# Unused matmuls of twelve kinds in front of every second feature-major block of a decoder trunk

## The chip, the cores and the metric

The kernel runs on one NeuronCore of a Trainium2 chip. The metric is the device time of one execution in microseconds (us); the median of three runs stands for a version.

## The reference

A trunk of two decoder layers on 256 positions of width 2048, all in float32. A layer is two residual steps:

```
proj  = rms_norm(x, norm1_w) @ w_in                 # 2048 -> 6400
mixed = [retention | dilated attention | gMLP]      # 768 + 768 + 512, each normalised
x     = x + mixed @ w_out                           # 2048 -> 2048
h     = rms_norm(x, norm2_w) @ w_up                 # 2048 -> 11264
x     = x + (silu(gate) * val) @ w_down             # conv of width 3 over h, 5632 -> 2048
```

A final RMSNorm follows the second layer. Nearly all arithmetic is in the four projections.

## The kernel before, in words

Every projection is done in three terms. An activation tile `x` is a float32r pair: `xh`, the rounded value, in columns 0 to 255, and `xl`, the remainder, in columns 256 to 511. A weight piece (128 rows x 1024 columns of float32) comes by DMA into `raw`; ScalarE writes its rounded part `hi` (L113) and VectorE the remainder `lo` (L123), both float32r. The product is hi·xh + hi·xl + lo·xh, three matmuls into one PSUM tile.

`proj_t` (L335 and after) computes feature-major blocks: one block is 128 output features by all 256 positions. For each of its 128-row slices k, `W.take` hands out the next 128 columns of `hi` and `lo`; these are the stationary operand, the 256 columns of `x` are the moving one, and L352 issues the three matmuls. So a block of w_out or w_up (16 slices) has 48 matmuls, and one of w_down has 48, 48 or 36 (three parts of 16, 16 and 12 slices). The first four blocks of a call (`lead`) are interleaved in groups of eight slices, as their inputs become ready; the others run one after the other. The accumulators are four PSUM tiles with the tag `mm`.

`proj_n` (L381 and after) does the position-major parts of w_in with the roles swapped: `x` is stationary, `hi` and `lo` are moving (L392).

All other matmuls of the kernel (attention, retention, gMLP, the sums of the norms, the transposes) write to a second set of four PSUM tiles, tag `mx`, got by `mx()`. They are slipped between two weight pieces of the main stream: at the start of each piece `W.take` calls `step`, which advances one stage of each waiting evacuation (`ev`) and of up to three background generators (`bg`), and splits the piece that will be needed three pieces later. The order on each engine is thus the order in which the Python program issues the instructions; there is no scheduler behind it. In plain float32 (not float32r) a matmul appears as two MATMUL instructions, each with its own weight load; a transpose and a float32r matmul appear as one.

The lines that the texts below name: L113 and L123 (the split of a weight piece), L352 (the feature-major stream), L392 (the position-major stream), L307 and L317 (sums and broadcast of a norm, float32, with `ones` and `diag`), L424 and L425 (attention scores, float32, 128 and 256 columns), L440 (transposes of attention), L447 to L449 (attention times values, float32, 128 columns), L410 (transposes of the mixer outputs), L479, L480 and L489 to L491 (retention). `ident` is a 128x128 identity and `ones` a 128x128 tile of ones, both float32.

Of the kernel before, what the change touches and what calls it, by code (L numbers as in the profile page):

```python
# [27 lines left out]
P = 128  # L28
D = 2048
S = 256  # L30
# [12 lines left out]
PIECE = 1024  # L43
# [27 lines left out]
class Weights:  # L71
# [48 lines left out]
    def split_lo(self, p, halves=(0, 1)):  # L120
        hi, lo, src = self.parts[p]
        for h in self._halves(p, halves):
            self.nc.vector.tensor_tensor(lo[:, h], src[:, h], hi[:, h].bitcast(F32), op=ALU.subtract)  # L123
        if p % PPC == PPC - 1 and 1 in halves:
            self.loaded.pop(p // PPC)
            if p >= 2:
                self.load(p // PPC + RAW + 1)

    def take(self, mat, l, row, col, width):
        p, off = divmod(self.pos, PIECE)  # L130
        if off == 0:
            new = list(range(self.nsplit, min(p + (self.ahead if p >= 8 else 2 if p else 1) + 1, self.npieces)))
            self.nsplit += len(new)
            if p < 8:
                for q in new:
                    self.split_hi(q)
                    self.split_lo(q)
                self.step(0)
                self.step(1)
            else:  # L140
                self.step(0)
                self.step(1)
                for q in new:
                    self.split_hi(q)
                    self.split_lo(q)
            self.parts.pop(p - 1, None)
        assert off + width <= PIECE
        self.plan.append((mat, l, row, col, width))
        self.pos += width
        hi, lo, _ = self.parts[p]  # L150
        return hi[:, off : off + width], lo[:, off : off + width]


def trunk_kernel(tc, x0, xt, stream, par, cst, wst, lnw, out):
# [3 lines left out]
    V, A, T, GP = nc.vector, nc.scalar, nc.tensor, nc.gpsimd  # L158
    ctx = ExitStack()
    with ctx:  # L160
# [38 lines left out]
        def run(g):  # L199
            ev.append(g)  # L200

        W = Weights(nc, stream, raw, hp, lp, 3, step)
        live = [0]

        def mm():
            until(lambda: live[0] < 4)
            live[0] += 1
            return ps.tile([P, 512], F32, name="mm", tag="mm")

        def mt():  # L210
            return mm()[:, 0:S]

        def mx():
            return ps.tile([P, 512], F32, name="mx", tag="mx")
# [16 lines left out]
        ident = cp.tile([P, P], F32, name="ident")  # L231
        make_identity(nc, ident)
        ones = cp.tile([P, P], F32, name="ones")
# [26 lines left out]
        def operand(j, wcol):  # L260

            w = first[:, j : j + 1] if wcol == C_N1 else prm[:, wcol + j : wcol + j + 1]
            p = pp.tile([P, 2 * S], F32R, name=f"p{j}", tag=f"p{j}")
            split_hi(p, X[j], w)
            yield
            split_lo(p, X[j], w)
            PX[j] = p
# [67 lines left out]
        def proj_t(mat, l, rows, cols, opnd, evac, lead):  # L335


            n = len(rows)
            groups = [list(range(lead))] + [[m] for m in range(lead, len(cols))]
            for g in groups:  # L340
                fast[0] = lead > 0 and W.pos > 0 and (len(g) > 1 or g[0] == len(cols) - 1)
                acc = {m: mt() for m in g}
                sz = 8 if len(g) > 1 else n
                for k0 in range(0, n, sz):
                    for m in g:
                        for k in range(k0, min(k0 + sz, n)):
                            x = opnd(k)
                            hi, lo = W.take(mat, l, rows[k], cols[m], P)
                            xh, xl = x[:, 0:S], x[:, S : 2 * S]
                            terms = ((hi, xh), (hi, xl), (lo, xh)) if l == 0 else ((hi, xh), (lo, xh), (hi, xl))  # L350
                            for i, (w, v) in enumerate(terms):
                                T.matmul(acc[m], w, v, start=k == 0 and i == 0, stop=k == n - 1 and i == 2)  # L352
                        if k == n - 1:
                            run(evac(m, acc[m]))

        def moved(acc):

            t = temp()
            A.activation(t, acc, AF.Copy)
            live[0] -= 1  # L360
            return t
# [44 lines left out]
        def mixed_block(slot, l, src, c0):  # L406

            t = mx()
            for j in range(2):
                T.transpose(t[:, j * P : (j + 1) * P], src[j][:, c0 : c0 + P], ident)  # L410
            q = qp.tile([P, 2 * S], F32R, name=f"q{slot}", tag=f"q{slot}")
            w = prm[:, C_MIX + l * NK + slot : C_MIX + l * NK + slot + 1]
            yield
            split_hi(q, t[:, 0:S], w)
            split_lo(q, t[:, 0:S], w)
            QX[slot] = q
# [189 lines left out]
        for l in range(DEPTH):  # L606
# [8 lines left out]
            def att_qk(m, acc):  # L615
# [3 lines left out]
                yield from scaled(acc, aqk[h][:, half * S : (half + 1) * S])  # L619

            proj_t("w_in", l, allrows, [c + h * P for h in range(H) for c in (AQ, AK)], p_of, att_qk, 4)
            fast[0] = False

# [18 lines left out]
            def ret_qk(m, acc):  # L642
# [12 lines left out]
                V.tensor_tensor(o, o, sw, op=ALU.add)  # L655

            proj_t("w_in", l, allrows, [c + h * P for h in range(H) for c in (RQ, RK)], p_of, ret_qk, 0)

            rv = pair("rv", 768)
# [28 lines left out]

            PX[:] = [None] * NK
            proj_t("w_out", l, MIX_ROWS, [m * P for m in range(NK)], q_of, ev_out(C_N2 + l * NK), 4)  # L690

            norm["ready"] = False
# [147 lines left out]
```

## Time and profile before

| | |
|---|---|
| median of three runs | 2307.31 us (2307.05 to 2308.6) |
| the profiled execution's own time | 2307.94 us |
| its span, first to last instruction | 2306.1 us |
| granted TensorE clock, mean | 0.998 |
| TensorE matmuls, weight loads | 19430 and 19430 |
| VectorE, ScalarE busy | 63% and 50% |

How to read it: PE is TensorE's matmul, PEld its weight load, DVE is VectorE, ACT ScalarE, POOL GpSimd, SP SyncE. Matmuls are pipelined: the time that one lasts (some 280 ns) is more than twice the time from one start to the next, so a sum of durations is no time of the stream. The chain that ended last gives, for each run of matmuls of one line, how long the stream stayed there; this time divided by the count is the step from matmul to matmul. Where the stream changes its line the boundary of two pieces of the chain can be off by a tenth of a microsecond.

### The profile page before, as it was taken

What the parts mean: (1) busy time and instruction counts of PE and PEld (TensorE: products, weight loads), DVE (VectorE), ACT (ScalarE), POOL (GpSimd) and SP (SyncE); (2) the same over time, 40 slices, a digit from 0 to 9 for tenths busy, and PEclk for the clock granted to TensorE, in tenths of its full rate; (3) what the DMA queues carried; (4) which work ended last, traced back from release to release, by engine and by line L of the source; (5) the groups of instructions that cost most, each with busy time, mean ns of one, the idle gap of its engine ahead of it and who ended that gap; (6) DMA issues with size and microseconds to landing.
All of it is one profiled execution on the core that took longest, in us unless ns stands there. A gap on an engine that the chain in (4) does not pass through costs nothing.

```text
span 2306.1 us, 45994 instructions
## 1 busy us (share of the span) xinstructions
PE 2288.8 (99%) x19430; PEld 2286.0 (99%) x19430; DVE 1444.7 (63%) x2086; ACT 1142.3 (50%) x1616; POOL 24.3 (1%) x38
## 2 busy tenths in 40 slices
PE   8999999999999999999999999999999999999998
PEld 8999999999999999999999999999999999999997
DVE  6465566677547775577655655667775577656765
ACT  6465555555435553455534645545544455434554
POOL 0000100000000000000000001000000000000000
PEclk9999999999999999999999999999999999999999
DMA  7545445555555555555555455555555555555553
GB/s 285 192 154 186 165 172 186 190 184 187 188 185 189 185 178 197 177 198 183 184 194 181 158 181 173 179 184 187 184 182 192 175 200 185 189 186 186 189 183 119
DMA packets 117135, 425.15 MB, mean 184 GB/s; under 512 B 12992, under 2 KB 12992, under 8 KB 116800
## 3 DMA queue, kind: packets, MB, share of 16 engines
q1 hardware_dynamic: 116928, 422.21, 53.5%
q8 instruction: 152, 2.49, 0.4%
q14 instruction: 55, 0.45, 0.1%
HBM read 420.06 MB, written 2.10 MB: 183 GB/s over the span
## 4 chain that ended last, share of the span: by engine, by line
PE 99%; DMA 0%; DVE 0%; SPq 0%; ACT 0%; POOLq 0%; issue 0%; DVEq 0%
PE mm L352 84%; PE mm L392 12%; PE mx L410 0%; DMA xg<-in_xt_dram 0%; PE mx L425 0%; PE mx L479 0%; DVE xg L750 0%; PE mx L307 0%; PE mx L440 0%; PE mx L544 0%; PE mx L490 0%; PE mx L449 0%; PE mx L448 0%; PE mx L491 0%; PE mx L489 0%; PE mx L480 0%
## 5 line engine op out<-in xcount | busy, mean ns | idle before, releaser
L123 DVE TENSOR_TENSOR lo<-raw,hi 128x1024 fp32r<-128x1024 f32 (+1 forms) x793 | 970.0, 1224 | 745.1 <-ACT hi L113 744.1
L113 ACT ACTIVATE hi<-raw 128x1024 fp32r<-128x1024 f32 (+1 forms) x793 | 836.7, 1057 | 920.6 <-PE mm L352 505.2
L352 PE MATMUL mm<-p,hi 128*128 128x256 f32 x7168 | 1280.4, 281 | 5.9 <-ACT hi L113 5.0
L352 PEld LDWEIGHTS mm<-p,hi 128*128 128x128 f32 x7168 | 1099.3, 188 | 7.1 <-ACT hi L113 5.0
L352 PE MATMUL mm<-p,lo 128*128 128x256 f32 x3584 | 1001.8, 280 | 0.0
L352 PE MATMUL mm<-q,hi 128*128 128x256 f32 x3840 | 679.9, 280 | 0.0
L352 PEld LDWEIGHTS mm<-p,lo 128*128 128x128 f32 x3584 | 673.6, 188 | 0.5 <-DVE lo L123 0.2
L352 PEld LDWEIGHTS mm<-q,hi 128*128 128x128 f32 x3840 | 586.4, 188 | 0.0
L352 PE MATMUL mm<-q,lo 128*128 128x256 f32 x1920 | 535.9, 279 | 0.0
L352 PEld LDWEIGHTS mm<-q,lo 128*128 128x128 f32 x1920 | 360.0, 187 | 0.0
L392 PE MATMUL mm<-hi,p 128*128 128x256 f32 x1664 | 270.3, 279 | 0.0
L392 PEld LDWEIGHTS mm<-hi,p 128*128 128x128 f32 x1664 | 230.1, 188 | 0.0
L392 PE MATMUL mm<-lo,p 128*128 128x256 f32 x832 | 178.8, 277 | 0.0
L714 ACT ACTIVATE a<-hs,prm 128x256 f32<-128x256 f32 x176 | 103.9, 590 | 64.0 <-DVE hs L366 64.0
L392 PEld LDWEIGHTS mm<-lo,p 128*128 128x128 f32 x832 | 133.2, 188 | 0.0
L717 DVE SCALAR_TENSOR_TENSOR a<-hs,prm,a 128x256 f32<-128x256 f32 x176 | 85.3, 485 | 6.3
L716 DVE SCALAR_TENSOR_TENSOR a<-hs,prm,a 128x256 f32<-128x256 f32 x176 | 84.3, 479 | 4.4 <-ACT a L714 4.4
L682 DVE TENSOR_TENSOR xg<-xg,mm 128x256 f32<-128x256 f32 x128 | 53.4, 418 | 49.0 <-PE mm L352 48.8
L366 DVE TENSOR_TENSOR hs<-mm,rbc 128x256 f32<-128x256 f32 x176 | 73.6, 418 | 3.4 <-PE mm L352 3.4
L720 ACT ACTIVATE a<-a 128x256 f32<-128x256 f32 x88 | 35.6, 404 | 30.4 <-DVE a L717 30.4
L276 ACT ACTIVATE t<-xg 128x256 f32<-128x256 f32 x75 | 30.1, 408 | 40.1 <-DVE xg L682 39.2
L726 ACT ACTIVATE q<-a 128x256 fp32r<-128x256 f32 x88 | 35.5, 403 | 3.5 <-DVE a L723 3.5
(119 smaller groups left out, 581.0 us busy)
## 6 DMA issues: line engine op xcount, KB each, us to landing
raw<-in_stream_dram SPq DMA_DIRECT2D x791, 512.0 KB, 3.5
out_dram<-xg SPq DMA_DIRECT2D x8, 256.0 KB, 2.4
xg<-in_xt_dram SPq DMA_DIRECT2D x3, 512.0 KB, 8.9
cs<-in_cst_dram SPq DMA_DIRECT2D x1, 1216.0 KB, 8.4
raw<-in_stream_dram SPq DMA_DIRECT2D x2, 256.0 KB, 4.0
ws<-in_wst_dram SPq DMA_DIRECT2D x2, 256.0 KB, 4.7
lw<-in_lnw_dram SPq DMA_DIRECT2D x2, 256.0 KB, 4.9
prm<-in_par_dram SPq DMA_DIRECT2D x1, 412.0 KB, 5.8
```

The costliest lines, as they stand in the source:

```text
L113: self.nc.scalar.activation(hi[:, h], src[:, h], AF.Copy)
L123: self.nc.vector.tensor_tensor(lo[:, h], src[:, h], hi[:, h].bitcast(F32), op=ALU.subtract)
L276: A.activation(sq, X[j], AF.Square)
L352: T.matmul(acc[m], w, v, start=k == 0 and i == 0, stop=k == n - 1 and i == 2)
L366: V.tensor_tensor(out, acc, norm["bc"], op=ALU.mult)
L392: T.matmul(acc[j][:, c], v, w[:, c], start=k == 0 and i == 0 and c.start == 0, stop=k == NK - 1 and i == 2, skip_group_check=True)
L682: V.tensor_tensor(X[m], X[m], acc, op=ALU.add)
L714: A.activation(a, hs[:, 2 : S + 2], AF.Identity, scale=conv_col(ch, 2), bias=conv_col(ch, 3))
L716: V.scalar_tensor_tensor(a, hs[:, 1 : S + 1], conv_col(ch, 1), a, op0=ALU.mult, op1=ALU.add)
L717: V.scalar_tensor_tensor(a, hs[:, 0:S], conv_col(ch, 0), a, op0=ALU.mult, op1=ALU.add)
L720: A.activation(a, a, AF.Silu)
L726: A.activation(q[:, 0:S], a, AF.Copy)
```

## The change

In `proj_t`, every block that is not of the lead group, whose index is even, and whose matrix is not w_in, gets one more matmul in front of its first one. Its kind is the next entry of the list `EXTRA`, 48 entries long, which is gone through round and round. The target is a new `mx` tile that nobody reads.

```
+    def piece(self):
+        return self.parts[(self.pos - 1) // PIECE][0]
...
+                if len(g) == 1 and mat != "w_in" and g[0] % 2 == 0:
+                    extra = EXTRA[nextra[0] % len(EXTRA)]
+                    nextra[0] += 1
+                else:
+                    extra = None
...
                             hi, lo = W.take(mat, l, rows[k], cols[m], P)
                             xh, xl = x[:, 0:S], x[:, S : 2 * S]
+                            if extra and k == 0:
+                                spare(extra, hi, x)
...
+        EXTRA = (2, -256, 128, 512, -1, 64, 320, -128, 192, 264, 384, 0)
+        EXTRA = EXTRA + EXTRA[::-1] + EXTRA[::2] + EXTRA[1::2] + EXTRA[::3] + EXTRA[1::3] + EXTRA[2::3]
+        nextra = [0]
+
+        def spare(n, hi, x):
+            t = mx()
+            if n > 0:
+                T.matmul(t[:, 0:n], hi, x[:, 0:n], start=True, stop=True)
+            elif n == 0:
+                T.transpose(t[:, 0:P], ident, ident)
+            elif n == -256:
+                T.matmul(t[:, 0:S], x[:, 0:P], W.piece()[:, 0:S], start=True, stop=True)
+            else:
+                T.matmul(t[:, 0 : -n], ident, ones[:, 0 : -n], start=True, stop=True)
```

A positive entry n takes the stationary `hi` that the block's first matmul takes too, and the first n of the 512 columns of `x` (float32r). -256 swaps the roles as `proj_n` does: 128 columns of `x` are stationary, the first 256 of the weight piece are moving. -1 and -128 are plain float32 with `ident` and 1 or 128 columns of `ones`; 0 is a transpose of `ident`.

## Rows read from the trace of the kernel before

**Rows 1.** The page: busy time by engine, and the granted clock in 40 slices

```profile
PE 2288.8 (99%) x19430; PEld 2286.0 (99%) x19430; DVE 1444.7 (63%) x2086; ACT 1142.3 (50%) x1616; POOL 24.3 (1%) x38
PEclk9999999999999999999999999999999999999999
```

**Rows 2.** Waits of TensorE: engine, line, waited for, us in total, times, longest

```profile
PE mm L352 <- ACT hi L113: 5.0, 1, 5.0
PE mx L317 <- DVE diag L314: 1.7, 1, 1.7
PE mm L352 <- ACT p L254: 0.9, 1, 0.9
PE mx L307 <- ACT t L276: 0.8, 1, 0.8
```

**Rows 3.** The chain, long pieces of the two main streams: start, length, line, matmuls

```profile
79.87 32.65 PE mm L392 x288
...
414.12 743.41 PE mm L352 x6312
...
1555.30 737.77 PE mm L352 x6264
```

**Rows 4.** The chain from 112 to 135 us, attention beside L352

```profile
116.00 0.22 PE mx L424 x2
116.22 0.43 PE mx L425 x2
...
119.48 0.22 PE mx L424 x2
119.70 0.43 PE mx L425 x2
120.14 2.83 PE mm L352 x24
122.97 0.33 PE mx L440 x3
123.29 2.73 PE mm L352 x24
126.02 0.33 PE mx L440 x3
126.35 2.83 PE mm L352 x24
```

**Rows 5.** The chain from 300 to 330 us, transposes of the mixer outputs

```profile
313.09 0.22 PE mx L410 x2
313.31 2.73 PE mm L352 x24
316.03 0.44 PE mx L410 x4
316.47 5.66 PE mm L352 x48
```

**Rows 6.** The chain in the second layer, after L440 and after L410

```profile
1264.47 2.73 PE mm L352 x24
...
1454.48 2.73 PE mm L352 x24
```

**Rows 7.** Weight loads in order of time around L307: start, length

```profile
409.70 0.30 PEld L307 LDWEIGHTS mx<-ones,sqacc 128*128 128x128 f32 x2
409.92 0.30 PEld L307 LDWEIGHTS mx<-ones,t 128*128 128x128 f32 x2
410.14 0.30 PEld L307 LDWEIGHTS mx<-ones,sqacc 128*128 128x128 f32 x2
410.37 0.30 PEld L307 LDWEIGHTS mx<-ones,t 128*128 128x128 f32 x2
410.59 0.30 PEld L352 LDWEIGHTS mm<-p,hi 128*128 128x128 f32 x2
```

**Rows 8.** One long stretch by engine: length, busy times, granted clock, DMA

```profile
420.00:1150.00 730.00, 730.00 (x6201) 730.00 (x6200) 480.75 (x684) 353.75 (x464) 0.00 (x0) 1.00 0.55 187
```

**Rows 9.** Groups of TensorE's instructions: line, form, count, busy, mean ns of one

```profile
L352 PE MATMUL mm<-p,hi 128*128 128x256 f32 x7168 | 1280.4, 281 | 5.9 <-ACT hi L113 5.0 <-ACT p L254 0.9
...
L440 PE MATMUL mx<-ident,s 128*128 128x128 f32 x36 | 5.9, 272 | 0.0
```

## The prediction
> **What bounds the kernel now.** Read the busy times first [rows 1]: TensorE's matmuls and its weight loads are both at 99%, VectorE at 63%, ScalarE at 50%, and the clock is full in every slice. Then the waits [rows 2]: TensorE waits 8.4 us in all, 5.0 of it for the first weight piece, and nothing in between but for the norms. So the time is a count of matmuls times a step, and the view that gives the step is the chain. Its long pieces [rows 3] show two different steps for matmuls of the same size: L352 goes at 743.41 / 6312 = 117.8 ns (and at 737.77 / 6264 = 117.8 in the second layer), L392 at 32.65 / 288 = 113.4. I call these the long and the short step. The 280 ns that one lasts [rows 9] is no step.
>
> The short step is no privilege of L392. After three transposes, L352 runs 24 matmuls in 2.73 us (113.8 each); three more transposes later, the next 24 take 2.83 (117.9) [rows 4]. It happens again at 313.31 [rows 5], and both come back at the same places of the second layer [rows 6]. In the whole chain L352 is resumed 48 times behind other matmuls, and these four times are the only ones with the short step. Nothing waits in these pieces, the clock is the same, the operands are the same: the stream has two rhythms, holds the one it has until something foreign stands in it, and after that may be in the other. In the long stretch it holds the long one through 6312 matmuls. This decides what the change is worth, since the change puts 124 foreign matmuls into just that stretch.
>
> **The count.** Blocks behind the lead group with an even index: 6 of w_out, 14 + 14 + 10 of w_up, 3 x 6 of w_down, 62 a layer, 124 in all. Two rounds of 48 and 28 more entries give 11 of each of 2, 128, -1 and 320, and 10 of each other kind. Nothing is removed; no DMA, no VectorE or ScalarE work is added.
>
> **The cost of each.** TensorE has no idle time to hide them, so each costs its own step.
> - 2, 64, 128, 192, 264 (52 of them): bound by the load of 128 weight columns. The nearest row is a one-column float32 matmul: two passes in 0.22 us, so 0.11 for a load with hardly anything streaming [rows 7]; from the other side the 256 columns at 0.118 [rows 3]. As weights and position are those of L352, I take 0.118: 6.1 us. At 0.110 it would be 5.7.
> - Per column: L425's pass is 0.215 us, L424's 0.110 with half as many columns [rows 4]. A float32 pass of 128 columns takes the time of 256 single-pass ones (the same 0.11 that L392 nearly needs for 256), so the 128 more are 256 column times in 0.105 us, 0.41 ns each. 264 columns are then 0.11 and stay under the load; 320 are 0.136 (11 of them, 1.5 us), 384 are 0.163 (10, 1.6 us), 512 are 0.216 as L425's pass (10, 2.2 us).
> - -256 is one L392 matmul, between 0.113 and 0.118: 10 x 0.116 = 1.2 us.
> - -1 and -128 are two passes: 0.22 each [rows 4, 7], 21 of them, 4.6 us.
> - 0 is one transpose: 0.33 / 3 = 0.11 [rows 4], 10 of them, 1.1 us.
>
> Sum: 6.1 + 1.5 + 1.6 + 2.2 + 1.2 + 4.6 + 1.1 = 18.3 us. The lower bound (every one-pass kind but the three wide ones at 0.110) is 17.7. The upper one comes from a doubt: no row shows a float32r matmul narrower than 256 columns. Should it go at the float32 rate of four column times, as L424's two passes do for 128 columns (0.22), then 128 costs 0.22 and 192 costs 0.32, in place of 0.118: 11 x 0.10 + 10 x 0.20 = 3.1 more, 21.4 us.
>
> A rule of the Trainium skill would make the narrow ones cheaper: "TensorE: Matmul & The Clock Gate", section "Back-to-back issue gap", has some 60 cycles (25 ns) for up to 64 columns and 134 cycles (56 ns) for 128. By it 2, 64 and 128 would save 32 x some 0.08 us, 2.5 us of the sum. The page calls this the isolated gap, without the weight load; the one-column passes of this trace, each with its load, stand 0.11 us apart [rows 7], so the trace does not agree for this stream. The same page, "Part 4: PE-mode transpose", puts a 128x128 transpose at about 275 ns in a kernel; that is what one lasts here too (272 ns [rows 9]), but its step is 0.11 [rows 4]. By 275 the ten would cost 1.7 us more.
>
> **Waits and buffers.** The extra matmul stands at a block's first slice, often at a piece's first columns, and takes over the wait for `hi`; the three matmuls behind it in TensorE's queue need the same `hi`. The stream waits for no weight piece after the start [rows 2], so nothing is late. The `mx` tile is free: in these stages only the two norms of a layer use that tag. The evacuations come 0.1 to 0.2 us later for VectorE and ScalarE, which are busy 481 and 354 of 730 us there [rows 8]. If the weight split were close behind the stream, TensorE would wait; at 66% it isn't.
>
> **What the rhythm gives back.** L352 matmuls from the first extra of a layer to the layer's end: 576 of w_out, 4224 of w_up, 2112 of w_down, 6912, twice 13824. Each is 4.4 ns shorter at the short step (117.8 - 113.4): 60.8 us if all were. Each extra stands in front of about 111 of them, worth 0.49 us, against its own price of 0.15. So the change breaks even where the short step holds in 18.3 / 60.8 = 30% of the stretch. The only estimate for that share which rows give is 4 of 48 resumptions, 8%: 5.1 us. Net 18.3 - 5.1 = 13.2 us. On the profiled execution's 2307.94 that is 2321.1; the median of the runs lies 0.6 lower, so I forecast 2320.
>
> **Rivals.**
> - *The narrow or the odd ones set the short step* (the other side). The 48 resumptions are all behind float32 matmuls or transposes, after which the stream changes its mode. Nine of the twelve kinds are float32r and leave the mode alone; a matmul whose stream ends long before the next load frees the two from each other, and -256 is of the kind in which L392 keeps the short step for 288 matmuls. If five of the twelve leave the short step behind, it holds in some 42%: 18.3 - 25.5 = -7, 2300. It decides from 30% on. For it: the long L352 piece is undisturbed, so no row says what such a matmul does to it. Against it: 44 of 48. Chance 0.18 for faster than break-even by over 4.6 us (a share over 38%).
> - *A draw*: a quarter to a third of the stretch goes at the short step, 18.3 - 0.29 x 60.8 = +1, 2309. Same reasons, one or two kinds fewer. Chance 0.22.
> - *Narrow float32r runs in four column times*: 21.4 - 5.1 = +16, 2324. For it: float32 does. Against: an instruction of 256 float32r columns shows one pass. Chance 0.08.
> - *It isn't there*: the unread results could be left out in the build. Then 2307.3. The kernel's lines are issued by hand and nothing reads them away. Chance 0.02.
>
> **How the numbers follow.** My forecast, the long step in most of the stretch (a share under 23%, from +18 to over +4.6 us, 2312 to 2326), has 0.50. The range: up, no short step at all gives 2325.6 and the float32 rate on top a little more, so 2327; down, it cuts into the first rival at a share of 45%: 18.3 - 27.4 = -9, 2298. About 0.2% (4.6 us) is what a measurement of this kernel can tell from no change. Slower by more: 0.50 + 0.08 = 0.58; within: 0.22 + 0.02 = 0.24; faster: 0.18.
>
> **What would show it.** The chain between 330 and 1155 us falls into pieces at each extra. Right: nearly all L352 pieces have 117.8 ns a matmul, the extras 0.11 to 0.22 us. Wrong in the price: steps behind 128 and 192 of over 0.2 us, or starts 25 ns behind the 2-column ones. Wrong in the rhythm: pieces of 96 matmuls in 10.9 us where the long step gives 11.3; then the kind in front of them tells which matmul sets the rhythm, and whether the same kind always does. Anything waited for in the stretch would refute the part on waits.

## The result, and the profile after

The changed kernel takes 2324.04 us (median of three, 2323.81 to 2324.54) where the kernel before took 2307.31: 16.7 us more, a ratio of 1.0071 (95% interval 1.0049 to 1.0094). I had forecast 2320, slower. The direction and its cause stand, but one term was three times too large, one kind of the list is never issued, and the thing I called a rhythm turned out to be worth more than the whole change: set on purpose, it makes the kernel 54 us faster than before. All times here are of executions at a granted clock of 0.997 or 0.998; one of six of the version with fourteen extras ran at 0.85 and took 2470.45 us, and it is left out.

The line of the changed kernel that answers to [rows 1] stands here; TensorE's waits are the four of [rows 2], 7.9 us in all, none of them in the stretch where the extras stand.

```profile
PE 2305.9 (99%) x19565; PEld 2301.9 (99%) x19565; DVE 1445.1 (62%) x2086; ACT 1143.0 (49%) x1616; POOL 25.2 (1%) x38
```

19565 - 19430 = 135 more matmuls. By form they are 83 of hi with x, 10 of x with hi, 22 of `ones` with one column, 20 with 128. No transpose is among them: `if extra and k == 0` is false for the kind 0. Ten of the 124 places are empty, so the change has eleven kinds, not twelve, and 114 extras.

The chain from 325 us on (start, length, line, matmuls; L362 is the stream that was L352, L374, L378 and L380 are the extras):

```profile
336.75 0.00 PE mx L374
336.75 11.41 PE mm L362 x96
348.16 0.12 PE mx L378
348.28 11.30 PE mm L362 x96
359.59 0.06 PE mx L374
359.64 11.36 PE mm L362 x96
371.00 0.24 PE mx L374
371.24 11.31 PE mm L362 x96
382.55 0.12 PE mx L380 x2
382.66 11.42 PE mm L362 x96
394.08 0.03 PE mx L374
...
440.89 0.22 PE mx L380 x2
441.11 10.89 PE mm L362 x96
451.99 0.09 PE mx L374
452.08 11.33 PE mm L362 x96
```

Each price is read from the start of one extra to the start of the next, since the border behind an extra is off by some 0.1 us. 96 long steps are 11.31 us. The 2-column extra and its 96 take 348.16 - 336.75 = 11.41, so it costs 0.10; -256 costs 0.12, 128 columns 0.10, 512 columns 0.24, -1 costs 0.22. Means over all extras of a kind, from the starts of the single matmuls in the trace: 2, 64, 128 and 192 columns 0.110 to 0.111 us, -256 0.116, 264 0.121, 320 0.145, 384 0.175, 512 0.237, -1 and -128 0.224. Times their counts (11 or 10) this is 17.4 us.

At 440.89 stands a float32 extra of 128 columns, and the 96 matmuls behind it take 10.89 us: 113.4 ns each, the short step of [rows 3 to 6]. Then the 192-column extra at 451.99 ends it. This happens four times in 114, three times behind -1 and once behind -128, with 360 matmuls in all: 360 x 4.44 ns = 1.6 us given back. 17.4 - 1.6 = 15.8; of the other 0.9 us, 0.3 is at the start (the first norm's matmuls at 33.59 us, before at 33.32) and 0.5 in the last broadcast (1.21 us, before 0.68), neither of them next to an extra.

### The profile page after: what moved, and what is told of

It reads as the page before. It is cut to its first block, busy times and chain, and to the rows that moved or that the text cites. A ratio compares the mean times of both kernels' runs of the same rounds, so it can differ in the third digit from the quotient of the medians.

```text
span 2322.8 us, 46250 instructions
## 1 busy us (share of the span) xinstructions
PE 2305.9 (99%) x19565; PEld 2301.9 (99%) x19565; DVE 1445.1 (62%) x2086; ACT 1143.0 (49%) x1616; POOL 25.2 (1%) x38
## 4 chain that ended last, share of the span: by engine, by line
PE 99%; DMA 0%; DVE 0%; SPq 0%; ACT 0%; POOLq 0%; issue 0%; DVEq 0%
PE mm L362 84%; PE mm L418 12%; PE mx L374 0%; PE mx L436 0%; DMA xg<-in_xt_dram 0%; PE mx L451 0%; PE mx L505 0%; DVE xg L776 0%; PE mx L310 0%; PE mx L466 0%; PE mx L570 0%; PE mx L380 0%; PE mx L320 0%; PE mx L517 0%; PE mx L474 0%; PE mx L475 0%
## 5 line engine op out<-in xcount | busy, mean ns | idle before, releaser
L362 PE MATMUL mm<-p,hi 128*128 128x256 f32 x7168 | 1287.7, 281 | 5.5 <-ACT hi L113 5.1
L362 PEld LDWEIGHTS mm<-p,hi 128*128 128x128 f32 x7168 | 1102.4, 188 | 7.2 <-ACT hi L113 5.1
L362 PE MATMUL mm<-p,lo 128*128 128x256 f32 x3584 | 1002.8, 280 | 0.0
L362 PE MATMUL mm<-q,hi 128*128 128x256 f32 x3840 | 684.6, 280 | 0.0
L362 PEld LDWEIGHTS mm<-p,lo 128*128 128x128 f32 x3584 | 674.0, 188 | 0.7 <-DVE lo L123 0.2
L362 PEld LDWEIGHTS mm<-q,hi 128*128 128x128 f32 x3840 | 588.4, 188 | 0.1
L362 PE MATMUL mm<-q,lo 128*128 128x256 f32 x1920 | 536.3, 279 | 0.0
L362 PEld LDWEIGHTS mm<-q,lo 128*128 128x128 f32 x1920 | 360.3, 188 | 0.0
L392 DVE TENSOR_TENSOR hs<-mm,rbc 128x256 f32<-128x256 f32 x176 | 73.6, 418 | 3.4 <-PE mm L362 3.4
```

What stands on the lines that cost most here:

```text
L392: V.tensor_tensor(out, acc, norm["bc"], op=ALU.mult)
```

## The experiments

**Parts of the change alone.** Same places and order, only one family of kinds issued.

```
-                    extra = EXTRA[nextra[0] % len(EXTRA)]
+                    kind = EXTRA[nextra[0] % len(EXTRA)]
                     nextra[0] += 1
...
+                    extra = kind if kind not in (-1, -128, 0) else None   # f32r_only
+                    extra = kind if kind in (-1, -128) else None          # f32_only
```

(The comments name the run that has the line; in both, `None` means no extra.)

> Only the 93 float32r extras of the change, at their places; the 21 float32 ones are left out. Theory (each extra costs its own step, and only float32 ones can bring the short step): prices read from the changed kernel are 0.110 us for 2, 64, 128 and 192 columns, 0.116 for -256, 0.121 for 264, 0.145 for 320, 0.175 for 384, 0.237 for 512; sum 12.7 us over the kernel before, and no piece of the stretch at the short step. Rival (float32r extras set the short step too, and the float32 ones among them took it away again): some pieces of 96 matmuls in 10.9 us, and under 12 us more than before.

Measured: 2320.54 us against 2307.53, ratio 1.0055 (1.0041 to 1.0069), 13.0 us more; no new piece at the short step. The theory of the prices is right to 0.3 us.

> Only the 21 float32 extras (-1 and -128) of the change, at their places. Theory (the stream holds the rhythm that it has until the next foreign matmul, and a float32 one leaves the short step behind in about one case of five): 21 x 0.224 = 4.7 us of price, but now some 660 L352 matmuls follow each, so that each short piece gives 2.9 us; four of them give 11.7 back: 7 us faster than before, with one short piece more or less moving it by 3. Rival 1 (the short step in L352 dies out by itself within a hundred matmuls or so): 4 x 0.4 = 1.7 back, 3 us slower than before. Rival 2 (the short pieces of the changed kernel came from the other extras around them): none, 4.7 us slower.

Measured: 2259.71 against 2307.53, ratio 0.9793 (0.9779 to 0.9806): 47.8 us *faster*. All three expected numbers were wrong, that of the theory included. The chain of this kernel shows why (L378 are its extras):

```profile
424.94 14.72 PE mm L362 x125
439.66 0.22 PE mx L378 x2
439.88 97.93 PE mm L362 x864
537.81 0.22 PE mx L378 x2
538.03 32.65 PE mm L362 x288
570.67 0.12 PE mx L378 x2
570.79 9.29 PE mm L362 x81
```

The extra at 439.66 brings the short step: 97.93 / 864 = 113.3 ns. The next ones, at 537.81 and 570.67, do *not* end it; the longest piece is 1152 matmuls in 130.57 us. Of the 21 extras, five met the long step and three of them left the short one; sixteen met the short step and all sixteen left it as it was. Behind the extras 11808 matmuls go short: 11808 x 4.44 ns = 52.4 us, less 21 prices of 0.225 = 4.7, gives 47.7. Only the norms' groups of float32 matmuls end it, at 1132.58 and 1526.01 us. So what kept the change slow was not that float32 extras seldom bring the short step, but that a float32r extra follows each and ends it.

**Which float32 groups bring it.** Groups in front of even blocks, the 320-column float32r extra in front of odd ones, behind the lead group throughout. In the names T is a transpose and N with a number a float32 matmul of so many columns.

```
+                    extra = 320
+                    if g[0] % 2 == 0:
+                        extra = EXTRA[nextra[0] % len(EXTRA)]
...
+        EXTRA = ("T", "TT", "N1", "N128", "TTT", "N2", "N1N1", "N256", "TTTT", "N64", "TN1")
```

> In front of every even block one of eleven float32 groups (1 to 4 transposes; one or two matmuls of 1, 2, 64, 128 or 256 columns; a transpose and a matmul), in a mixed order, and in front of every odd block the 320-column float32r extra, which ended the short step each time that it met it. Theory (whether the stream comes out short depends on where in a fixed grid of time the group ends, so on its length and on where the stream stands): no kind always, some kinds in a third or more of their 11 places, others never; on the whole 15 to 30 of the 124 blocks behind a group at 113.3 ns a matmul, all 124 blocks behind a 320 at 117.8. Rival (a float32 group of any kind draws the rhythm with the same odds, one in five): all kinds between 0 and 5 of 11.

Measured: short behind 28 of 124 groups: one matmul of 1, 2 or 64 columns 6 of 11 each, of 128 columns 3 of 12, three transposes 3 of 11, two transposes and TN1 2 of 11 each; never behind one or four transposes, two one-column matmuls, or 256 columns. The kinds are not alike, as the rival had it. That their length decides is argued, not shown: one matmul of 1 column and one of 128 both take 0.22 us and brought it 6 of 11 and 3 of 12 times. The 320-column extra ended all 28.

**Which float32r widths bring it.** The same places, with a width from a list in front of even blocks and 320 columns in front of odd ones.

```
+        EXTRA = (322, 330, 326, 334, 324, 332, 328)      # survey_width
+        EXTRA = (312, 336, 344, 352, 360, 392, 296)      # survey_16
```

> In front of every even block a float32r extra of 322, 324, 326, 328, 330, 332 or 334 columns in a mixed order, in front of every odd block one of 320. 16 columns are the 6.67 ns in which the starts of the stream come round (three long steps are 353.3 ns, 53 x 6.67; one short one 113.3, 17 x 6.67). Theory (the start of the next matmul within these 6.67 ns decides): a wide extra sets that start by its columns, so one or two of the seven widths leave the short step behind nearly every time and the others never; blocks of 48 then in 5.44 us, not 5.65. Rival (only a change between float32 and float32r can bring the short step): no block at the short step, all seven widths alike but for 0.42 ns a column.

```profile
643.59 0.14 PE mx L374
643.74 5.65 PE mm L363 x48
649.39 0.15 PE mx L374
649.54 5.44 PE mm L363 x48
654.98 0.14 PE mx L374
655.12 5.65 PE mm L363 x48
```

The extra at 649.39 has 328 columns: 5.44 us for 48, the short step. 328 did so in 17 of 18 places; the miss, at 429.97 us, is the only one of them with a norm between it and the 320-column extra before it. The six other widths did so in none of 106. Two columns more or less, 0.8 ns at the 0.41 ns a column of [rows 4], decide here, and the rival (only a change of type can do it) is refuted.

> As the survey of widths, with 312, 336, 344, 352, 360, 392 and 296 columns in front of the even blocks and 320 in front of the odd ones. Theory (what counts is the columns modulo 16, as 16 columns are 6.67 ns): 312, 344, 360 and 392, which are 8 more than a multiple of 16 as 328 is, leave the short step behind in nearly all their places; 336 and 352 never do; 296 is 8 more too, but its stream of 0.123 us is hardly longer than a long step, so it may be set by the load instead and fail. Rival (328 is special by itself): none of them does.

Measured: 312 columns bring the short step in 17 of 17 places; 344, 360 and 392 never (0 of 54), nor 336, 352 and 296. So "columns modulo 16" holds for 312 and 328 and fails above them and at 296, which had been given a reason to fail. What singles these two out stays open.

**328 in front of every even block.**

```
+                extra = 328 if len(g) == 1 and mat != "w_in" and g[0] % 2 == 0 else None
```

> 328 columns in front of every even block, 124 of them, where the change has its mixed list. Theory (the start within the 6.67 ns decides; 328 columns carry the start of the long step onto that of the short one, and so must carry the short one's off it): the pieces between extras alternate, one at 113.3, the next at 117.8; prices 0.137 and 0.157; 18 of price, 30 given back, 2295. Rival (328 columns leave the short step behind whatever was before): all pieces at 113.3, 17 of price, 60 back, 2265.

Measured: 2313.70 us, ratio 1.0025 (1.0015 to 1.0035), 6.2 us slower: neither number. The prices are 0.150 each in this trace, 18.6 in all, and the 2976 matmuls behind the hits give 13.2 back. The chain (L365 are the extras) shows a turn of four:

```profile
529.74 0.15 PE mx L365
529.89 11.31 PE mm L358 x96
541.20 0.15 PE mx L365
541.35 10.88 PE mm L358 x96
552.23 0.14 PE mx L365
552.38 11.31 PE mm L358 x96
563.68 0.15 PE mx L365
563.84 11.31 PE mm L358 x96
575.14 0.15 PE mx L365
```

The extra of 541.20 brings the short step, that of 552.23 ends it, and two more find and leave the long one before the next hit: 32 hits, 32 ends, 60 misses. The same width in the same place of the loop does three things, in order, and the pieces in front of a hit and of a miss have the same 117.8 ns. So the long step is not one state; three would make this turn of four. That there are just three, one for each position of a slightly longer step (118.3 beside 117.5 and 117.5 ns) within the three matmuls of a slice, is argued from the single starts, not shown.

**328 once where it should last.** Extras at the listed pairs (call of `proj_t` in the layer, block) only: call 0 is the first projection, 2 is w_out, 3 the first part of w_up. A hit is an extra that leaves the short step behind.

```
+                if len(g) == 1 and (ncall[0] % 9, g[0]) in ((0, 5), (2, 4), (3, 4)):                                   # six_328
+                if len(g) == 1 and (ncall[0] % 9, g[0]) in ((0, 5), (0, 6), (0, 7), (2, 4), (3, 4), (3, 6), (3, 8)):   # fourteen_328
```

> No extras but three a layer, each of 328 columns (float32r, hi stationary): in front of block 5 of the first projection, of block 4 of w_out, and of block 4 of the first part of w_up, which is the first lone block behind the matmuls of the norm. Theory (328 columns set the short step from the long one, and it then holds until the next foreign matmul): 113.3 ns a matmul from there to the next norm or mixer work, some 14200 matmuls at 4.4 ns less, six prices of 0.14: 2307.5 - 62 = 2246, the bound known for this stretch. Rival (the short step needs to be set again and again, as the fifteen or so float32 extras of the run without float32r did): short only for some hundred to thousand matmuls behind each: 2260 to 2300. Rival 2 (set in a survey block behind a 320 only, not from the undisturbed stream): 2308.

Measured: 2306.45 against 2307.46, ratio 0.9995 (0.9986 to 1.0004): no difference. Only the w_out extras hit (624 matmuls in 70.72 us in each layer, up to the next norm); the other four left the long step, which then ran through 6192 and 6144 matmuls. The 1248 short ones give 5.5 us; six prices take 0.9, and the L408 pieces behind the first projection (L392 before) lose 1.3 in each layer:

```profile
40.95 39.57 PE mm L360 x336
80.52 33.92 PE mm L408 x288
```

In front of these 288 stand 336 long steps and no foreign matmul. In the kernel before it is the same, with 360 long steps (42.40 us from 37.47 on), but there the 288 take 32.65 us [rows 3]. An extra that missed has still changed something: two streams at the same 117.8 ns went on differently. The short step lasts without help, but one extra does not reach it from everywhere.

> Seven extras of 328 columns a layer: in front of blocks 5, 6 and 7 of the first projection, of block 4 of w_out, and of blocks 4, 6 and 8 of the first part of w_up. In the run with 328 in front of every even block, behind the norm the first two missed (steps 117.8) and the third met; the run with six shows the same first miss at both places and a hit in w_out. Theory (the long step has three positions against the triple of matmuls, 328 carries the stream from the first to the second to the third to the short step): short from the third one on and held to the next norm, some 13600 matmuls at 4.4 ns less and 14 prices of 0.14 to 0.15: 59 us faster, 2248. Rival (the order of misses and hits in that run hung on its own earlier extras): w_out alone is gained, 5.5 - 2.1 = 3 us, 2304.

Measured: 2252.87 (median of five) against 2307.01, ratio 0.9763 (0.9750 to 0.9777): 54.1 us faster, the best of all versions, where 59 had been expected. The same kernel was run once more:

> The kernel with fourteen extras once more, for a trace at the full clock: its runs were 54 us faster than before where 59 were expected. Theory: the pieces behind the third extra of each w_up stand at 113.3 ns a matmul to the next norm (53 us), and the 5 us are missing at the small places, one or both of the first projections or of w_out at 117.8. Rival: all places are met, and the short step itself dies out somewhere in the long pieces, which would then show more than 113.4 ns a matmul on the mean.

Measured: this one execution took 2251.19, 56.3 less than the kernel before beside it.

```profile
78.54 33.92 PE mm L408 x288
336.67 70.72 PE mm L360 x624
448.74 680.00 PE mm L360 x6000
1191.64 33.92 PE mm L408 x288
1304.67 32.65 PE mm L408 x288
1449.77 70.72 PE mm L360 x624
1561.85 674.58 PE mm L360 x5952
```

680.00 / 6000 is 113.33 ns: short for 6000 matmuls on end, where [rows 3] had 117.8, so the rival is refuted. Every place hit at the extra foreseen: the third of three behind each norm and in each first projection, the one in w_out. The theory looked for the missing 5 us at the wrong place, though. 13680 short matmuls give 60.8, fourteen prices take 2.0; and the L408 piece behind the first projection runs at 33.92 / 288 = 117.8 here too: 2 x 1.27 = 2.5 lost. 60.8 - 2.0 - 2.5 = 56.3, this execution's gain. That accounts for half of the 5 us; the other 2.2 lie between this execution and the median of the five, and no trace shows them.

**Each kind from the short step.** The blocks behind the lead groups in turns of three: 320, 328, a kind of the change.

```
+                    extra = (320, 328)[c] if c < 2 else EXTRA[(ncall[0] // 3 - 1) % len(EXTRA)]
```

> Every lone block of w_out, w_up and w_down has an extra, in turns of three: 320, 328, then one of the eleven kinds of the change, so that each kind meets the stream at the short step about seven times. Theory (a float32r extra moves the next start off the one place where the short step holds, a float32 one lets the stream stand and start anew on it): behind -1 and -128 the short step goes on every time, behind all nine float32r kinds it is 117.8. Rival (any foreign matmul ends the short step as often as it brings it): -1 and -128 end it in four of five cases. Third possibility: a narrow float32r kind, which costs less than a step, keeps it too; then the change's loss would hang on the wide ones alone.

```profile
612.05 5.44 PE mm L362 x48
617.49 0.06 PE mx L373
617.54 5.71 PE mm L362 x48
623.25 0.15 PE mx L373
...
646.69 5.44 PE mm L362 x48
652.13 0.12 PE mx L377 x2
652.25 5.55 PE mm L362 x48
657.80 0.14 PE mx L373
```

The float32r extra at 617.49 has the long step behind it (623.25 - 617.49 = 5.76 = 0.11 + 5.65). The float32 one at 652.13 has the short one (5.67 = 0.23 + 5.44). In all, 2, 64, 128, 192, 264 and 384 columns met the short step seven or eight times each and ended it every time (44 of 44); -1 and -128 met it seven times each and kept it every time. -256 and 512 never met it here, nor did 320 among the kinds; but as the first of the turns and in the three surveys 320 ended 76 of 76. The rival is out, and there is no cheap float32r keeper among those met; of the theory, what -256 and 512 do stays untried. They met no short step because the 328 in front of them never hit. In this run 328 hit in 59 of 83 places, and the misses have an order: it missed in all 23 turns behind a 2-, 64- or 128-column extra, and once behind a norm; in the other 59 it hit. A 320-column extra and two blocks of long steps stand between, so the long step carries on something of what came two extras earlier.

## Why the prediction was right, and where not

- *What bounds the kernel, and the two rhythms*: right. All but 0.9 us was found in steps of the stream, nothing in new waits; both rhythms were in the trace before. That a stream holds its rhythm until something foreign comes is right with one addition: the mere change from the feature-major to the position-major line shifts it too, from long to short before (at 79.87) and from short to long with fourteen extras (at 78.54).
- *The count*: wrong by ten. I read the branches of `spare` and not the condition in front of the call. "It isn't there" was a rival for the whole, and was true for a twelfth.
- *The cost of each*: 18.3 forecast, 17.4 measured; without the ten transposes my sum is 17.2. The narrow ones cost 0.110 to 0.111, as much as the one-column passes of [rows 7], not my 0.118. The wide ones cost more than my 0.41 ns a column: 0.145, 0.175 and 0.237 for 0.136, 0.163 and 0.216; why is not shown. Four column times for narrow float32r is refuted: 128 and 192 columns cost what 2 do. That 2 and 64 cost as much as 192 shows a bound that does not depend on columns. The Trainium skill, "TensorE: Matmul & The Clock Gate", section "LDWEIGHTS (loading the stationary operand)", gives a weight load in ns as its columns / 1.2, so an estimated 107 ns for 128; the measured 110 to 111 ns agree within 4%. The 25 ns of its section "Back-to-back issue gap" for up to 64 columns, which the prediction had set aside, do not show: 2 columns cost 0.110 us here.
- *What the rhythm gives back*: the mis-sized term. I took 8%, from 4 resumptions of 48; it was 360 of 13824 matmuls, 2.6%: 1.6 us for 5.1. Two things were mixed in that share. How often an extra brings the short step: 4 of 114. And how long it then lasts: no further than the next float32r extra, and 93 of 114 are that. The rows of before held only float32 matmuls and transposes, so the second could not be read there.
- *The rival on the other side* had its mechanism right and its kinds wrong. I gave the narrow float32r ones the power to set the short step; they never did and always ended it. The float32 ones, which I had counted against it with "44 of 48", hold it. Had the list contained only those, the change would have been faster by 47.8 us, far outside my range. That my forecast held is in part luck: 93 of the 114 extras are float32r, and those that met the short step ended it, which nothing in the prediction foresaw.

The 4 of 48 was also misread. Two of the four resumptions, at 313.31 and 1454.48, did not bring the short step; they found it in L392 and kept it:

```profile
307.63 5.46 PE mm L392 x48
313.09 0.22 PE mx L410 x2
313.31 2.73 PE mm L352 x24
```

5.46 / 48 is 113.8 ns, in front of the transposes. So L352 was brought from the long step to the short one in 2 of 40 resumptions; L392, which I did not count, came out short in 10 of its 20. In the change it was 4 of the 21 float32 extras and none of the 93 others.

The forecast of 13.2 for 16.7 is thus 0.9 too much in prices, 3.5 too much given back by the rhythm, and 0.9 at start and end, which I had not in the sum.

## What to carry to other kernels

In a stream that nothing waits for, divide long pieces of the chain by their counts; if equal matmuls show two steps, the slower one may be a rhythm that a single matmul can shift, and the price of an insertion is then not only its own time but also what it does to the thousands behind it. Ask of every inserted instruction two things separately: what it does to a stream in the one state, and in the other. Read the condition that issues an instruction as closely as the instruction.

## What the runs showed of the hardware

- Equal float32r matmuls (128x128 by 256 columns) with a weight load each run at 113.33 ns (680.00 us / 6000) or at 117.78 (743.41 / 6312), at the same granted clock (1.00 in both stretches), and hold either for 6000 on end. One short step is 17 x 6.667 ns, three long ones are 53 x 6.667 ns; 16 columns at the 0.41 ns of [rows 4] are about as much, an estimate. That something with this period decides fits the widths that differ by 16 (312 and 328) but not 296, 344 and 360; what it is stays open.
- Which of the two it is can depend on 0.8 ns: in one survey 328 columns bring the short step in 17 of 18 places, 326 and 330 in none of 35. It depends as well on what came before: 328 hit in 32 of 92 places where it met the long step in front of every even block, and in 59 of 83 in turns of three.
- One float32 matmul of 1 or 128 columns (two passes, 0.22 us) left the short step standing in 30 of 30 cases. A norm's four in a row ended it in 7 of 7, and in the kernel before so did the three transposes at 126.02 us [rows 4]. A float32r one ended it in 156 of 156, at every width that met it (2 to 384 columns).
